# Second feed-forward: the first two feature tiles of the up projection by eight plain products, the differences of token blocks built after them

## The chip, the cores and the metric

The kernel runs on one core of one Trainium2 chip. The core has TensorE (PE, matrix products into PSUM; PEld is its weight load), VectorE (DVE), ScalarE (ACT), GpSimd (POOL) and SyncE (SP, which issues nearly all transfers here). They run side by side, each through its own instructions in order, and wait for one another by semaphores. The metric is device time in microseconds (us).

## The reference

Two layers of a hybrid attention trunk over 1024 latent tokens (plus 256 context tokens) of width 1024: the first with neighbourhood attention, the second with sliding-window attention. Each layer ends with a gated feed-forward with a convolution over positions. In the second layer only the latent tokens pass through it:

```python
def conv_ffn(h, w_up, conv_w, conv_b, w_down):
    u = h @ w_up
    u_p = jnp.pad(u, ((0, 0), (CONV_W // 2, CONV_W // 2), (0, 0)))
    u = sum(u_p[:, tap:tap + t] * conv_w[tap] for tap in range(CONV_W)) + conv_b
    a, g = jnp.split(u, 2, axis=-1)
    return (a * jax.nn.silu(g)) @ w_down
...
h = modulate(rmsnorm(x, g_ffn[i]), sh2, sc2)
x = x + gt2 * conv_ffn(h, ffn_w_up[i], ffn_conv_w[i], ffn_conv_b[i], ffn_w_down[i])
```

D_FF is 2816, so `w_up` has 2 x 2816 columns: 22 feature tiles of 128, each with an `a` and a `g` half.

## The kernel before

**Storage and precision.** Activations lie with the feature on the 128 partitions and tokens along the row: eight slices k of 128 features (0 to 3 are the upper half of the width, 4 to 7 the lower), each 128x512 for one of two token blocks (0: tokens 0 to 511, 1: the rest). Products are made in a reduced format, with each operand split into a high part (a rounded copy, ScalarE) and a low part (the rest, VectorE), and three matmuls for each slice: high by high, high by low, low by high.

**The up projection.** For a feature tile the four results (`a` and `g`, token blocks 0 and 1) are a 2x2 by 2x2 block product: the weights `R["a"]` and `R["g"]` in two halves of 512 rows, and the normalised input in two halves (slices 0 to 3 and 4 to 7) for two token blocks. A plain way takes eight products of 4 slices each. The kernel takes seven, in Strassen's manner (`PROD`, lines 1676 and 1677): it multiplies sums and differences of weight halves by sums and differences of input blocks, and combines the results. In order these are b11, b21, t2, t3, t1, t4, b22; they go into the banks a, d, a, c, a, c, a. `b11` and `b21` are block 0's own two halves; `b22` is block 1's lower half; t1 to t4 are differences (lines 1629 to 1651). Each product is 4 slices x 3 matmuls of 128x512. `plan_up` (from line 1681) also loads the raw weights, forms the four weight sums S1 to S4 (VectorE), splits four weight operands p = 0 to 3 (`plan_w`), copies the first products from PSUM into c0 and c1 (ScalarE), adds the later ones onto them (`out_p`, VectorE), and then forms the convolution (a centre tap on ScalarE, two taps on VectorE for each of g and a), the gate, and combined blocks for the down projection, which go out to DRAM.

**The order.** All work of a feed-forward is handed to a planner (`Sched`, line 61) as operations with an engine, a due key, reads, writes, and claims on rings of buffers. The planner fixes the order on each engine when the kernel is built: among the ready operations the lowest key goes first. A claim in one ring by operations of one class is taken in the order in which the operations were planned. Rings that matter here: `x` (8 buffers of 128x1024: the block 1 input takes 4 of them, c0, c1 and two u the rest), `raw` (3, raw weights from DRAM and the modulation weights `wm`), `w` (4 pairs of split weights), `sr` (4), and 8 banks of PSUM.

**The stretch in question** lies at the start of the second layer's up projection. Ahead of it PE does the attention's output projection (`plan_oproj`) for token block 1; each of the eight results is added to the residual, squared and summed. Then comes the norm of block 1 (`plan_sums`, `plan_bc`: a short chain PE mp, DVE n1v, POOL n1y, DVE n1t, n1y, nsum, PE bc, ACT nsum). `plan_t` multiplies slices by the norm and scale, and lines 1629 to 1663 build t1 to t4 and b22 from both blocks, with high parts on ScalarE and low parts on VectorE (`parts`). Their results lie in tiles t12, t34 and b22. At the same time four steps of the modulation product of the last gate (`plan_mod`, line 354, tile `mod`) are done, with eight loads `wm`. Names in rows: `ua`, `uc`, `ud` are PSUM banks of the up projection, `b1` block 0's split slices, `wraw` raw weights, `whi`/`wlo` split ones, `s` weight sums, `u` and `c` the convolution's tiles.

Of the kernel before, what the change touches and what calls it, by code (L numbers as in the profile page):

```python
# [226 lines left out]
def trunk_kernel(ctx, tc, xperm, xseq, cc, wmod, bmod, gnorm, na_wqkv, na_gq, na_gk, na_bias, na_wo,  # L227
# [3 lines left out]
    act, dve, pool, pe, dma = [InOrder(tc, e) for e in (nc.scalar, nc.vector, nc.gpsimd, nc.tensor, nc.sync)]  # L231
# [35 lines left out]
    dsh = spool.tile([P, 104], F32, name="dsh")[:, :8]  # L267
# [538 lines left out]
    with tc.tile_pool(name="x0", bufs=1, reuse_waits="tile") as xp, \  # L806
# [5 lines left out]
        h = [hi_lo("h0", 0), None, hi_lo("h0", 2)]  # L812
# [4 lines left out]
        for c, parts, key in ((2, 2, 0), (0, 4, 2), (1, 4, 30)):  # L817
            t0, n = CH[c]
# [9 lines left out]
        for kt in range(KT):  # L828
# [110 lines left out]
        for j in range(4):  # L939
# [15 lines left out]
    def ps_alloc(pool_):  # L955
# [6 lines left out]
                bias=3, osb=2, v=8, vc=4, q=8, qc=2, kkc=2, klc=2)  # L962
# [10 lines left out]
    def pair(a):  # L973
# [127 lines left out]
    bias = {}  # L1101
# [158 lines left out]
    FTS = [ft + NP * k for ft in range(NP) for k in range(2)]  # L1260

    def ffn(l, opj, xt1, todo):
        last = l == 1
# [7 lines left out]
        sc = Sched(dict(b=8, raw=3, w=WBUFS, x=8, sr=SRB, g=GB, g2=GB, sq=2), {"b", "raw", "w", "x", "sr", "g", "g2", "sq"})  # L1271
# [22 lines left out]
        LO = {n: ("dve", t_dve(n) + 0.03) for n in (512, 1024)}  # L1294
# [3 lines left out]
        X = [None] * 3  # L1298
# [144 lines left out]
        shift, scale = [modc[:, l, 0, v, :] for v in (3, 4)]  # L1443
        Nm = {}
# [173 lines left out]
        def parts(c, k, hi, lo, tok, key, rel, reads=()):  # L1618
            sc.op("act", t_act(512), lambda e: act.activation(hi(), X[c][:, k, :], AF.Copy), reads=[("x", c, k)] + list(reads),
                  writes=[tok + ("h",)], key=key, rel=rel)  # L1620
            sc.op("dve", t_dve(512), lambda e: sub(e, lo(), X[c][:, k, :], hi().bitcast(F32)), reads=[("x", c, k), tok + ("h",)],
                  writes=[tok + ("l",)], key=key, rel=rel)

        def stt(c, k, c0, k0, s, c1, k1):

            return lambda e: dve.scalar_tensor_tensor(out=X[c][:, k, :], in0=X[c0][:, k0, :], scalar=s, in1=X[c1][:, k1, :],
                                                      op0=ALU.add, op1=ALU.subtract)
        tst = t_dve(512) + 0.06
        for step in range(3):
            for j in range(4):  # L1630
                key = kb + (30.0 * j + 4 * step if not last else 2.0 * j + 8 * step)
                sh = shift[:, j + 4:j + 5]
                if step == 0:
                    plan_t(1, 512, Nm[1], j, xap(1), xtok(1), scale, key)
                    sc.op("dve", t_dve(512), lambda e, j=j: dve.tensor_tensor(
                        out=X[0][:, j, :], in0=X[1][:, j, :], in1=X[0][:, j, :], op=ALU.subtract), reads=[("x", 1, j)],
                        writes=[("x", 0, j)], key=key)
                    parts(0, j, lambda j=j: t12h()[:, 2 * j, :], lambda j=j: t12l(j)[:, 0, :], ("t1", j), key, ())
                elif step == 1:
                    plan_t(1, 512, Nm[1], j + 4, xap(1), xtok(1), scale, key)  # L1640
                    sc.op("dve", tst, stt(0, j, 1, j + 4, sh, 0, j), reads=[("x", 1, j + 4)], writes=[("x", 0, j)], key=key,
                          rel=rx(1, j + 4))
                    parts(0, j, lambda j=j: t12h()[:, 2 * j + 1, :], lambda j=j: t12l(j)[:, 1, :], ("t2", j), key, rx(0, j))
                else:
                    sc.op("dve", tst, stt(1, j, 1, j + 4, dsh[:, j:j + 1], 1, j), reads=[("x", 1, j + 4), ("dsh",)],
                          writes=[("x", 1, j)], key=key, rel=rx(1, j + 4))
                    parts(1, j, lambda j=j: t34_(0)[:, j, :512], lambda j=j: t34_(1)[:, j, :512], ("t3", j), key, rx(1, j), hcs)
                    sc.op("dve", tst, stt(0, j + 4, 0, j + 4, sh, 0, j), reads=[("x", 0, j)], writes=[("x", 0, j + 4)], key=key,
                          rel=rx(0, j))
                    parts(0, j + 4, lambda j=j: t34_(0)[:, j, 512:], lambda j=j: t34_(1)[:, j, 512:], ("t4", j), key, rx(0, j + 4),  # L1650
                          hcs)

        hold = [("hcu",)] if not last else [("t4", j, "l") for j in range(4)]
        sc.op("x", 0.0, lambda e: None, reads=hold, writes=[("hcfree",)], key=-100)
        for j in range(4):
            key = kb + (30.0 * j + 12 if not last else 2.0 * j + 24)
# [4 lines left out]
            sc.op("dve", tst, lambda e, j=j, k=k: dve.scalar_tensor_tensor(  # L1661
                out=b2l()[:, j, :], in0=X[1][:, k, :], scalar=shift[:, k:k + 1], in1=b2h()[:, j, :].bitcast(F32), op0=ALU.add,
                op1=ALU.subtract), reads=[("x", 1, k), ("b2", j, "h")], writes=[("b2", j, "l")], key=key, rel=rx(1, k))

        BP = dict(
            b11=(lambda j: (b1h()[:, j, :], b1l(j // 2)[:, j % 2, :]), lambda j: ("b1", j)),
# [1 line left out]
            b22=(lambda j: (b2h()[:, j, :], b2l()[:, j, :]), lambda j: ("b2", j)),  # L1670
            t1=(lambda j: (t12h()[:, 2 * j, :], t12l(j)[:, 0, :]), lambda j: ("t1", j)),
            t2=(lambda j: (t12h()[:, 2 * j + 1, :], t12l(j)[:, 1, :]), lambda j: ("t2", j)),
            t3=(lambda j: (t34_(0)[:, j, :512], t34_(1)[:, j, :512]), lambda j: ("t3", j)),
            t4=(lambda j: (t34_(0)[:, j, 512:], t34_(1)[:, j, 512:]), lambda j: ("t4", j)))

# [5 lines left out]
        def plan_up(pos):  # L1681
# [33 lines left out]
            ra, rg = T("r", "a"), T("r", "g")  # L1715

            sc.op(*ADD, lambda e: s_op(e, 1, 0, True, lambda: R["g"][:, :512], lambda: R["g"][:, 512:], ALU.add),
                  reads=[rg],
# [953 lines left out]
```

## Time and profile before

| | us |
|---|---|
| median of 3 runs (2808.72 to 2809.52) | 2808.81 |
| the profiled execution | 2809.03 |
| its span on the core | 2807.3 |
| second up projection, first product at | 2147.68 |
| first product of the down projection behind it at | 2587.74 |

Times in rows are us from the start of the span. "Busy" of PE counts matmuls from issue to a modelled end, so that successive ones overlap; the distance of two starts is the real price. Nearly every row carries L51, the line of the helper that records each operation, so rows are told apart by tiles.

### The profile page before, as it was taken

To read this page: it belongs to the slowest core of one execution; us is meant where nothing else is said; L and a number is where in the kernel's file an instruction comes from. 1 tells how busy PE (TensorE), PEld (TensorE's weight loads), DVE (VectorE), ACT (ScalarE), POOL (GpSimd) and SP (SyncE) were. 2 spreads that over 40 slices of the span, in tenths; PEclk is the share of its full clock that TensorE was granted. 3 is DMA by queue.
4 is the path that set the end of the run, shared out by engine and by line. 5 is a ranking of instruction groups with operands and counts; after the bars stand their busy time and mean duration, and the time that the engine had idled before them with its cause. 6 is when DMAs were issued, how large, how long until landed. Compare 5 with 4: busy or idle time off the path is not lost.

```text
span 2807.3 us, 45623 instructions
## 1 busy us (share of the span) xinstructions
PE 2755.6 (98%) x16205; PEld 2426.1 (86%) x16205; DVE 2281.2 (81%) x4990; ACT 1689.7 (60%) x3315; POOL 413.6 (15%) x675
## 2 busy tenths in 40 slices
PE   6999999999999999999999999999999999999999
PEld 5999999999889987777788879999987788888887
DVE  7888878889688687877787688888988888888757
ACT  5877777778456554445454457888864555545443
POOL 1222212223000000000000007645430000000000
PEclk9999999999999999999999999999999999999999
DMA  6232222224645543444466561100253332334745
GB/s 251 65 98 81 66 76 83 89 77 136 242 143 188 187 166 134 161 147 145 152 226 224 166 222 39 30 18 20 82 203 131 121 109 94 113 112 143 251 150 180
DMA packets 144293, 373.52 MB, mean 133 GB/s; under 512 B 22080, under 2 KB 35008, under 8 KB 142656
## 3 DMA queue, kind: packets, MB, share of 16 engines
q1 hardware_dynamic: 144064, 370.60, 39.5%
q8 instruction: 127, 2.08, 0.3%
q14 instruction: 102, 0.84, 0.1%
HBM read 303.50 MB, written 67.04 MB: 132 GB/s over the span
## 4 chain that ended last, share of the span: by engine, by line
PE 70%; DVE 3%; ACT 1%; DMA 1%; issue 1%; POOL 0%; DVEq 0%; SPq 0%; ACTq 0%
PE ua L51 17%; PE dn L51 15%; PE uc L51 13%; PE mm L51 6%; PE ud L51 4%; PE oacc L51 4%; PE pt L51 3%; PE pv L51 3%; PE s L51 2%; PE dnc L51 2%; PE mod L51 1%; DVE S L51 1%; DVE x L51 0%; DVE wlo L51 0%; DVE ptlo L51 0%
## 5 line engine op out<-in xcount | busy, mean ns | idle before, releaser
L51 ACT ACTIVATE whi<-wraw 128x512 fp32r<-128x512 f32 (+1 forms) x264 | 212.3, 805 | 202.6 <-PE uc L51 61.5
L51 DVE TENSOR_TENSOR wlo<-wraw,whi 128x512 fp32r<-128x512 f32 (+1 forms) x264 | 239.3, 908 | 45.2 <-ACT whi L51 44.6
L51 DVE TENSOR_TENSOR ptlo<-pt,pthi 128x512 fp32r<-128x512 f32 (+2 forms) x384 | 223.4, 596 | 56.2 <-ACT pthi L51 53.1
L51 PE MATMUL dn<-ghi,whi 128*128 128x512 f32 x616 | 243.8, 396 | 0.0
L51 PE MATMUL dn<-ghi,wlo 128*128 128x512 f32 x616 | 242.8, 394 | 0.0
L51 PE MATMUL dn<-glo,whi 128*128 128x512 f32 x616 | 242.0, 393 | 0.0
L51 ACT ACTIVATE S<-S,m 128x640 f32<-128x640 f32 (+3 forms) x288 | 221.0, 769 | 26.4 <-DVE m L51 22.6
L51 ACT ACTIVATE pthi<-pt 128x512 fp32r<-128x512 f32 (+2 forms) x384 | 195.3, 524 | 65.0 <-PE pt L51 57.3
L51 DVE SCALAR_TENSOR_TENSOR u<-c,cv,u 128x1023 f32<-128x1023 f32 x176 | 223.2, 1280 | 6.9 <-ACT u L51 5.8
L51 ACT ACTIVATE whi<-s 128x1024 fp32r<-128x1024 f32 (+1 forms) x120 | 113.1, 943 | 190.8 <-PE uc L51 137.2
L51 ACT ACTIVATE ghi<-graw 128x512 fp32r<-128x512 f32 x154 | 96.4, 630 | 192.2 <-PE dn L51 112.5
L51 PE MATMUL pt<-idr,S 128*128 128x128 f32 x1280 | 194.6, 273 | 2.4 <-DVE ptlo L51 1.0
L51 PE MATMUL mm<-whi,h0hi 128*128 128x384 f32 x512 | 181.6, 355 | 0.4 <-ACT qraw L51 0.4
L51 DVE TENSOR_TENSOR glo<-graw,ghi 128x512 fp32r<-128x512 f32 x154 | 105.5, 688 | 82.9 <-ACT ghi L51 76.5
L51 PE MATMUL mm<-wlo,h0hi 128*128 128x384 f32 x512 | 172.3, 337 | 0.0
L51 DVE TENSOR_TENSOR wlo<-s,whi 128x1024 fp32r<-128x1024 f32 (+1 forms) x120 | 129.6, 1080 | 42.4 <-ACT whi L51 42.2
L51 PEld LDWEIGHTS pt<-idr,S 128*128 128x128 f32 x1280 | 151.0, 140 | 10.0 <-DVE ptlo L51 1.7
L51 POOL TENSOR_TENSOR n1y<-n1v,mhalf 128x4 f32<-128x4 f32 (+1 forms) x9 | 9.2, 1024 | 934.7 <-DVE n1v L51 934.7
L51 PE MATMUL ua<-t12hi,whi 128*128 128x512 f32 x352 | 138.7, 394 | 5.5 <-ACT t12hi L51 4.0
L51 POOL TENSOR_TENSOR qy<-qv,mhalf 128x4 f32<-128x4 f32 (+1 forms) x112 | 119.6, 1069 | 149.4 <-DVE qv L51 129.3
L51 PEld LDWEIGHTS dn<-ghi,wlo 128*128 128x128 f32 x616 | 115.5, 187 | 28.4
L51 PEld LDWEIGHTS dn<-glo,whi 128*128 128x128 f32 x616 | 115.5, 188 | 27.4
(353 smaller groups left out, 8767.0 us busy)
## 6 DMA issues: line engine op xcount, KB each, us to landing
wraw<-in_w_up_dram SPq DMA_DIRECT2D x132, 512.0 KB, 3.5
wm<-in_wmod_dram SPq DMA_DIRECT2D x80, 512.0 KB, 4.1
wraw<-in_w_down_dram SPq DMA_DIRECT2D x44, 512.0 KB, 3.6
graw<-g_dram SPq DMA_DIRECT2D x44, 512.0 KB, 4.5
wraw<-in_w_down_dram SPq DMA_DIRECT2D x88, 256.0 KB, 3.1
graw<-g_dram SPq DMA_DIRECT2D x66, 256.0 KB, 2.8
slab<-in_na_wqkv_dram SPq DMA_DIRECT2D x32, 384.0 KB, 3.7
woraw<-in_na_wo_dram SPq DMA_DIRECT2D x24, 512.0 KB, 4.0
```

Of the source, the lines that this page charges most:

```text
L51: r = f(*a, **k)
```

## The change

It affects the second layer only (`PLAIN = 2 if last else 0`). Tiles 0 and 1 (`pos < PLAIN`) are made by eight plain products, four banks U[s, n] (s: a or g; n: token block), with two raw weights split whole and no sums of weights; each result leaves PSUM by one copy on ScalarE and there are no additions onto c. The products of block 0 (n = 0) read b11 and b21 as before. Those of block 1 (n = 1) read new split slices `e` of block 1, which `early` writes into the tiles of t3 and t4. The differences are planned after these two tiles, with keys later by 8; t3 and t4 wait until the last plain products have read `e` (`done`). The normalisation of block 1's slices moves from the differences into `early`. `plan_u`, the convolution and what follows, is the old code as a function of its own.

```diff
-        for step in range(3):
+        PLAIN = 2 if last else 0
+        done = [[("up", FTS[p], "done", h, j) for p in range(PLAIN) for j in range(4)] for h in range(2)]
+
+        def early(h, key):
             for j in range(4):
...
+                k = 4 * h + j
+                cs = slice(512 - 512 * h, 1024 - 512 * h)
+                plan_t(1, 512, Nm[1], k, xap(1), xtok(1), scale, key + j)
+                sc.op("act", t_act(512), lambda e, j=j, k=k, cs=cs: act.activation(
+                    t34_(0)[:, j, cs], X[1][:, k, :], AF.Identity, bias=shift[:, k:k + 1]),
+                    reads=[("x", 1, k)], writes=[("e", h, j, "h")], key=key + j)
+                sc.op("dve", tst, lambda e, j=j, k=k, cs=cs: dve.scalar_tensor_tensor(
+                    out=t34_(1)[:, j, cs], in0=X[1][:, k, :], scalar=shift[:, k:k + 1], in1=t34_(0)[:, j, cs].bitcast(F32),
+                    op0=ALU.add, op1=ALU.subtract), reads=[("x", 1, k), ("e", h, j, "h")], writes=[("e", h, j, "l")], key=key + j)
...
+        if PLAIN:
+            early(0, kb)
+            early(1, kb + 4)
+        def plan_diffs():
+            for step in range(3):
+                for j in range(4):
+                    key = kb + (30.0 * j + 4 * step if not last else 2.0 * j + 8 * step + 8 * (PLAIN > 0))
...
+                        parts(1, j, lambda j=j: t34_(0)[:, j, :512], lambda j=j: t34_(1)[:, j, :512], ("t3", j), key, rx(1, j), hcs + done[1])
...
+                        parts(0, j + 4, lambda j=j: t34_(0)[:, j, 512:], lambda j=j: t34_(1)[:, j, 512:], ("t4", j), key, rx(0, j + 4),
+                              hcs + done[0])
...
-                sc.op("dma", 1.8, load, writes=[T("r", s)], key=pk - 8, acq=[("raw", T("r", s), 5 if s == "a" else 4)])
+                sc.op("dma", 1.8, load, writes=[T("r", s)], key=pk - 8, acq=[("raw", T("r", s), 2 if pos < PLAIN else 5 if s == "a" else 4)])
...
+            if pos < PLAIN:
+                for p, r, s in ((0, ra, "a"), (3, rg, "g")):
+                    w = ("up0" if p == 0 else "up", ft, "w", p)
+                    sc.op("act", t_act(1024), whi(p, lambda s=s: R[s], 1024), reads=[r], writes=[T("w", p, "h")], key=pk + p,
+                          acq=[("w", w, 16)], rel=[r])
+                    sc.op(*LO[1024], wlo(p, lambda s=s: R[s], 1024), reads=[r, T("w", p, "h")], writes=[T("w", p, "l")], key=pk + p,
+                          rel=[r])
+                U, C = {}, {}
+                for n in range(2):
+                    for kh in range(2):
+                        for s in range(2):
+                            p = 3 * s
+                            ap, tok = BP[f"e{kh}" if n else f"b{kh + 1}1"]
+                            for j in range(4):
+                                def mm(e, s=s, p=p, kh=kh, n=n, j=j, ap=ap):
+                                    if kh == 0 and j == 0:
+                                        U[s, n] = bank(f"u{s}{n}")
+                                    hi, lo = ap(j)
+                                    ws = slice(512 * kh + j * P, 512 * kh + (j + 1) * P)
+                                    for m, (w, x) in enumerate(((0, hi), (0, lo), (1, hi))):
+                                        pe.matmul(U[s, n], W[p][w][:, ws], x, start=(kh == 0 and j == 0 and m == 0),
+                                                  stop=(kh == 1 and j == 3 and m == 2))
+                                tk = tok(j)
+                                sc.op("pe", 3 * t5, mm, reads=[T("w", p, "h"), T("w", p, "l"), tk + ("h",), tk + ("l",)],
+                                      writes=[T("u", s, n)] + ([T("done", kh, j)] if s and n else []),
+                                      key=key + (2.72 * (2 * kh + s) if n == 0 else 10.9 + 5.44 * kh + 1.36 * j + 0.68 * s),
+                                      acq=[("b", ("u", s, n, ft), 1)] if kh == 0 and j == 0 else (),
+                                      rel=[("up0" if p == 0 else "up", ft, "w", p)])
+                    for s in range(2):
+                        def out(e, s=s, n=n):
+                            if n == 0:
+                                C[str(s)] = x_tile("c" + str(s))
+                            act.activation(C[str(s)][:, 512 * n:512 * n + 512], U[s, n], AF.Copy)
+                        sc.op("act", t_actp(512), out, reads=[T("u", s, n)], writes=[T("c", 2 * s + n)], key=key - 30,
+                              acq=[("x", T("ct", s), 3)] if n == 0 else (), rel=[("u", s, n, ft)])
+                plan_u(pos, ft, key, C, T)
+                return
...
+            plan_u(pos, ft, key, C, T)
+
+        def plan_u(pos, ft, key, C, T):
             V = {}
...
         for pos in range(FT):
+            if pos == PLAIN:
+                plan_diffs()
             plan_up(pos)
```

More of the change, by code (lines that the diff above doesn't have):

```diff
@@ L1653, in ffn @@
[L1653 to L1656, printed above, removed]
+                k = 4 * h + j
[4 more added lines that the diff above has]
+                    reads=[("x", 1, k)], writes=[("e", h, j, "h")], key=key + j)
@@ L1657, in ffn, with b22 @@
+                sc.op("dve", tst, lambda e, j=j, k=k, cs=cs: dve.scalar_tensor_tensor(
+                    out=t34_(1)[:, j, cs], in0=X[1][:, k, :], scalar=shift[:, k:k + 1], in1=t34_(0)[:, j, cs].bitcast(F32),
+                    op0=ALU.add, op1=ALU.subtract), reads=[("x", 1, k), ("e", h, j, "h")], writes=[("e", h, j, "l")], key=key + j)
+        def b22(j, key):
             k = j + 4
@@ L1663, in ffn @@
                 op1=ALU.subtract), reads=[("x", 1, k), ("b2", j, "h")], writes=[("b2", j, "l")], key=key, rel=rx(1, k))
+        if PLAIN:
[5 more added lines that the diff above has]
+                    key = kb + (30.0 * j + 4 * step if not last else 2.0 * j + 8 * step + 8 * (PLAIN > 0))
+                    sh = shift[:, j + 4:j + 5]
+                    if step == 0:
+                        if not PLAIN:
+                            plan_t(1, 512, Nm[1], j, xap(1), xtok(1), scale, key)
+                        sc.op("dve", t_dve(512), lambda e, j=j: dve.tensor_tensor(
+                            out=X[0][:, j, :], in0=X[1][:, j, :], in1=X[0][:, j, :], op=ALU.subtract), reads=[("x", 1, j)],
+                            writes=[("x", 0, j)], key=key)
+                        parts(0, j, lambda j=j: t12h()[:, 2 * j, :], lambda j=j: t12l(j)[:, 0, :], ("t1", j), key, ())
+                    elif step == 1:
+                        if not PLAIN:
+                            plan_t(1, 512, Nm[1], j + 4, xap(1), xtok(1), scale, key)
+                        sc.op("dve", tst, stt(0, j, 1, j + 4, sh, 0, j), reads=[("x", 1, j + 4)], writes=[("x", 0, j)], key=key,
+                              rel=rx(1, j + 4))
+                        parts(0, j, lambda j=j: t12h()[:, 2 * j + 1, :], lambda j=j: t12l(j)[:, 1, :], ("t2", j), key, rx(0, j))
+                    else:
+                        sc.op("dve", tst, stt(1, j, 1, j + 4, dsh[:, j:j + 1], 1, j), reads=[("x", 1, j + 4), ("dsh",)],
+                              writes=[("x", 1, j)], key=key, rel=rx(1, j + 4))
+                        parts(1, j, lambda j=j: t34_(0)[:, j, :512], lambda j=j: t34_(1)[:, j, :512], ("t3", j), key, rx(1, j), hcs + done[1])
+                        sc.op("dve", tst, stt(0, j + 4, 0, j + 4, sh, 0, j), reads=[("x", 0, j)], writes=[("x", 0, j + 4)], key=key,
+                              rel=rx(0, j))
+                        parts(0, j + 4, lambda j=j: t34_(0)[:, j, 512:], lambda j=j: t34_(1)[:, j, 512:], ("t4", j), key, rx(0, j + 4),
+                              hcs + done[0])
+            sc.op("x", 0.0, lambda e: None, reads=[("hcu",)] if not last else [("t4", j, "l") for j in range(4)],
+                  writes=[("hcfree",)], key=-100)
+            for j in range(4):
+                b22(j, kb + (30.0 * j + 12 if not last else 2.0 * j + 24))
@@ L1715, in plan_up @@
             ra, rg = T("r", "a"), T("r", "g")
+            if pos < PLAIN:
[11 more added lines that the diff above has]
+                            ap, tok = BP[f"e{kh}" if n else f"b{kh + 1}1"]
+                            for j in range(4):
+                                def mm(e, s=s, p=p, kh=kh, n=n, j=j, ap=ap):
[21 more added lines that the diff above has]
+                return
```

23 lines of the change are left out of this document (2 added, 21 removed).

## The prediction

> **What bounds the kernel now.** I read the page's first part, then stretches of the second feed-forward's start, then TensorE's waits there.
>
> ```profile
> span 2807.3 us, 45623 instructions
> PE 2755.6 (98%) x16205; PEld 2426.1 (86%) x16205; DVE 2281.2 (81%) x4990; ACT 1689.7 (60%) x3315; POOL 413.6 (15%) x675
> ```
>
> PE is busy for 98% of the span, so only a place where PE waits, or fewer products, can shorten it. The next view cuts the up projection of the second layer into stretches (columns: stretch, length, then busy time and instructions of PE, PEld, DVE, ACT, POOL; granted clock; DMA share; GB/s).
>
> ```profile
> 2147.68:2156.16 8.48, 7.43 (x41) 6.13 (x40) 5.65 (x15) 2.92 (x4) 1.01 (x1) 1.00 0.38 125
> 2156.16:2162.10 5.94, 5.85 (x27) 4.33 (x25) 5.78 (x10) 1.77 (x3) 0.00 (x0) 1.00 0.28 91
> 2162.10:2167.20 5.10, 1.15 (x17) 0.42 (x16) 5.10 (x9) 2.84 (x4) 0.00 (x0) 0.92 0.60 198
> 2167.20:2176.70 9.50, 8.51 (x29) 4.34 (x30) 9.50 (x16) 3.15 (x5) 0.00 (x0) 0.51 0.24 74
> 2176.70:2191.60 14.90, 14.90 (x77) 11.39 (x75) 13.36 (x21) 9.93 (x15) 0.00 (x0) 1.00 0.31 101
> 2191.60:2198.70 7.10, 4.42 (x31) 2.86 (x31) 6.32 (x7) 5.88 (x7) 0.00 (x0) 1.00 0.62 214
> 2207.10:2226.14 19.04, 19.04 (x86) 15.77 (x85) 17.51 (x21) 10.04 (x13) 0.00 (x0) 1.00 0.34 125
> 2226.14:2587.70 361.56, 361.56 (x1597) 299.49 (x1596) 298.45 (x346) 184.70 (x225) 0.00 (x0) 1.00 0.31 109
> ```
>
> The seventh row is one feature tile of seven products: 19.04 us, so 2.72 a product. From 2207 on PE is full. Ahead of that it is not, and in the third and fourth rows DVE is busy for all 14.6 us: it builds the differences of token blocks that the products t2, t3, t1, t4 need. The clock there is 0.51. TensorE's waits in this place name the chain:
>
> ```profile
> PE ua L51 <- ACT t12hi L51: 4.0, 1, 4.0
> PE ua L51 <- ACT c L51: 1.4, 1, 1.4
> PE mod L51 <- ACT modsb L51: 1.2, 1, 1.2
> PE bc L51 <- DVE nsum L51: 1.0, 1, 1.0
> PE ua L51 <- DVE t12lo L51: 0.9, 2, 0.5
> ```
>
> PE's timeline has the ends of the stage and what lies in it besides products (start, duration, engine, line, operation, then idle time ahead and its releaser):
>
> ```profile
> 2147.68 0.39 PE L51 MATMUL ua<-b1hi,whi 128*128 128x512 f32 x1
> ...
> 2151.09 0.95 PE L51 MATMUL mp<-invd,nsum 128*128 128x1 f32 x8
> 2151.90 0.48 PE L51 MATMUL ud<-b1hi,whi 128*128 128x512 f32 x1
> ...
> 2155.25 1.16 PE L51 MATMUL bc<-nsum,ones 128*128 128x128 f32 x8 [1.05 <-DVE nsum L51]
> 2156.16 0.48 PE L51 MATMUL ua<-b1hi,whi 128*128 128x512 f32 x1
> ...
> 2162.18 1.07 PE L51 MATMUL mod<-wm,cpad 128*32 128x256 f32 x16
> ...
> 2167.21 0.79 PE L51 MATMUL ua<-t12hi,whi 128*128 128x512 f32 x1 [3.96 <-ACT t12hi L51]
> ...
> 2587.74 0.40 PE L51 MATMUL dn<-ghi,whi 128*128 128x512 f32 x1
> ```
>
> The up projection runs from 2147.68 to 2587.74, 440.06 us. 22 tiles of 19.04 are 418.88. The norm's two small steps take 0.81 and 0.91 (start to start of the next), four modulation steps of 1.07 take 4.28, their transpose some 0.2 (my estimate): 6.2. What is left, 440.06 - 418.88 - 6.2 = 15.0 us, is loss, all ahead of 2198.7. Its pieces: 4.0 waiting for t12hi; in the fourth row 9.5 us in which only 12 product matmuls (2.72) and one modulation step (1.07) ran, so 5.7 lost to the clock and two waits for t12lo; 1.4 for c; 1.2 for modsb; 1.0 for nsum; 1.7 in small change. These 15.0 us are all that the change can win.
>
> **The change, part by part.** Removed from tiles 0 and 1: the seven products each on differences. Added: eight plain ones each. The first four (n=0) need only token block 0 and the raw weights, which are split before 2147.68 or soon after; the other four (n=1) need the eight slices e of block 1. So PE has 2 x 8 x 2.72 = 43.52 us instead of 38.08: **+5.44 us**, on the path for certain.
>
> What it buys is order. DVE's prices, from the same stretch and from the steady one (line, engine, operation, shapes, count, busy, mean ns, idle ahead), and its pitch from two successive starts:
>
> ```profile
> L51 DVE SCALAR_TENSOR_TENSOR x<-x,modc,x 128x512 f32<-128x512 f32 x8 | 5.9, 742 | 0.0
> L51 DVE TENSOR_TENSOR t12lo<-x,t12hi 128x512 fp32r<-128x512 f32 x8 | 5.2, 682 | 0.0
> L51 DVE SCALAR_TENSOR_TENSOR b22lo<-x,modc,b22hi 128x512 fp32r<-128x512 f32 x4 | 2.8, 748 | 0.1
> L51 DVE SCALAR_TENSOR_TENSOR u<-c,cv,u 128x1023 f32<-128x1023 f32 x76 | 96.3, 1279 | 0.1
> L51 DVE TENSOR_TENSOR u<-u 128x1024 f32<-128x1024 f32 x19 | 23.1, 1218 | 0.1
> ...
> 2157.08 1.41 DVE L51 SCALAR_TENSOR_TENSOR x<-x,modc,nsum 128x512 f32<-128x512 f32 x2 [0.16 <-ACT nsum L51]
> 2158.41 1.29 DVE L51 TENSOR_TENSOR x<-x,x 128x512 f32<-128x512 f32 x2
> 2159.61 0.74 DVE L51 SCALAR_TENSOR_TENSOR x<-x,modc,nsum 128x512 f32<-128x512 f32 x1
> ```
>
> Two of the three-operand form take 1.33 start to start, two of the plain form 1.20: 0.66 and 0.60 each. By the same overlap of about 0.08 a 1024-wide one is 1.14 and a tap of the convolution 1.20.
>
> *The slices e.* Eight normalisations and eight low parts, 16 x 0.66 = 10.6 us of DVE from 2157.1 to 2167.7; ScalarE's eight high parts run beside them. They stand first by their keys (46 to 53, against 54 to 78 for the differences). PE reaches them after 10.88 us of n=0 products, 1.72 of norm steps, and the wait for nsum: about 2161.6, or 2162.7 with one modulation step. The first slice is there by about 2160.2 (one normalisation, ScalarE's 0.63 as for the 128x512 split below, one low part, two hand-overs). DVE delivers a slice every 1.33 us and PE uses one every 1.36: no wait. The 4.0 and the 5.7 go.
>
> *Tile 1's n=0* is another 10.88 us that needs no difference, so the differences have from 2167.7 until tile 1's end, T1. T1 is 2147.68 + 43.52 + 6.2 + waits of about 1.5 = 2198.9.
>
> *DVE's bill from 2167.7 to T1*, 31.2 us: first differences and t1 low parts 8 x 0.60 = 4.8; t2 with low parts 4 x (0.66 + 0.60) = 5.0; tile 0's four taps, product and one block 4 x 1.20 + 1.14 + 0.60 = 6.5; of tile 2's weights two low parts and four sums 2 x 1.14 + 4 x 0.60 = 4.7; the eight sums for t3 and t4 5.3. That is 26.3, or 28.7 with t4's low parts. It fits, at some 90% of DVE's time. Against this the plain tiles spare DVE eight weight sums, two weight splits, and six additions onto c; these were on no path of PE's.
>
> *The added wait.* t3 and t4 take the same tile as e1 and e0, so their high parts wait on ScalarE for the last n=1 products ("done"): t4 from 5.44 us before T1, t3 from T1 on. Behind T1 tile 2 wants t3 at T1 + 8.16, t4 at 13.6, b22 at 16.3. There DVE owes t3's low parts 2.4, tile 1's taps 4.8, one weight split 1.14, an addition 0.60: 8.9 us from about T1 + 1.3, done by T1 + 10.2 at worst with t3's first slices earlier. Then b22 2.65, tile 1's product and three blocks 2.9, one split 0.60: 16.4. Nearly in time, nothing over.
>
> *The x ring* is what is late next. Block 1's four buffers of eight are kept until t3 and b22 are split, now behind T1; tile 1 has the other four (c0, c1 and two u). Tile 2's c0 must be copied out before its third product may go on in the same bank, at T1 + 5.44. A buffer comes free when tile 1's first part has had both taps. ScalarE's prices here:
>
> ```profile
> 2188.84 0.63 ACT L51 ACTIVATE whi<-wraw 128x512 fp32r<-128x512 f32 x1 [1.29 <-PE uc L51]
> 2189.79 1.24 ACT L51 ACTIVATE u<-c,cv 128x1024 f32<-128x1024 f32 x1 [0.32 <-DVE c L51]
> 2191.79 0.60 ACT L51 ACTIVATE c<-ua 128x512 f32<-128x512 f32 x1 [0.75 <-PE ua L51]
> ```
>
> Copy of the last bank done at T1 + 1.5 (one weight split in front of it), the centre tap to 3.2, two taps on DVE to 5.8, copy of tile 2's c0 to 6.4, PE at 6.7: 1.3 late. One slice of t3 (0.68) can fill part. I take 0.9; bounds are 0 (the order there lets the copy through) and 3.5 (second centre and both parts' taps stand in front).
>
> *Waits that stay:* nsum 1.0, as that chain is not changed, with 0.2 about it; bounds 0.6 (the addition onto c that stood in the chain is gone) and 1.2. modsb 1.2 is an order that the planner may or may not repeat: 0.6, bounds 0 and 1.2. Small change 0.3, bounds 0 and 1.7. The loads I cost at nothing: raw buffers of the plain tiles are free after two uses instead of five, so the eight modulation loads, which now begin at 2149.26 and queue for one buffer, get more of them, and tile 2's follow by about 2175, 24 us ahead of T1. If that cover fails PE waits for a load, 3.5 us.
>
> ```profile
> wraw<-in_w_up_dram SPq DMA_DIRECT2D x132, 512.0 KB, 3.5
> ...
> 2139.96 0.33 SPq L51 DMA_DIRECT2D wraw<-in_w_up_dram  x1
> ...
> 2149.26 36.54 SPq L51 DMA_DIRECT2D wm<-in_wmod_dram  x8
> ```
>
> **Sum:** 15.0 - 5.44 - (1.2 + 0.6 + 0.9 + 0.3 = 3.0) = 6.6 us won. From the profiled execution's 2809.03 that gives 2802.4; the median of the runs is 0.22 lower, so **2802.2 us**. The best case by the lower bounds (0.6 left) wins 9.0: 2799.8. From 2198 on PE waits for nothing, so what is won there arrives at the end whole.
>
> The 0.51 of the fourth stretch follows the idle 3.96 us, while the other waits, up to 1.4 us, left the clock at 1.00. The Trainium skill, "TensorE: Matmul & The Clock Gate", Part 1, says that the array falls to half speed after about one idle window of 3.4 us and wants one such window of work to come back. The trace agrees as to 0.51 and to the side of 3.4 on which each wait lies; by that page a wait of 1 or 2 us behind T1 costs itself alone, and one past 3.4 brings a slow stretch along; the page alone changes no term of the sum.
>
> **The rivals.**
>
> *The gain is half eaten behind T1.* The x ring and t3 cost their upper 3.5, modsb 1.2, small change 1.7, nsum 1.2: 7.6 left in place of 3.0, so 2.0 won: 2806.8. For it: DVE has no slack from 2157 on, and three things wait for tile 1's end at once. Against it: the part that frees the buffer has a low key.
>
> *The stall moves and returns whole (slower).* If DVE's work, 54 us from 2157.1 to b22's low parts at T1 + 16.3 = 2215.2 (10.6 + 26.3 + 8.9 + 2.4 for t4 + 6.2), runs at the steady stretch's 298.45/361.56 = 83% instead of 93%, it takes 65 us, 7 us too long. PE then waits 7 in tile 2, which is longer than the 3.96 that was followed by a slow stretch losing 5.7. Left: 3.0 - 0.9 + 7 + 5.7 = 14.8; with the 5.44 that is 20.2 against 15.0 before: 2814.0. It becomes slower than before once the new wait, with its slow stretch, passes 15.0 - 5.44 - 2.1 = 7.5, so already from one unbroken wait of about 4. For it: in-order engines and a 90% bill. Against it: DVE was busy 14.6 of 14.6 us in the old stall, so it can run dense, and the 83% of the steady stretch is lack of work.
>
> *The cover is not there.* Tile 1's banks are claimed after tile 0's in a fixed turn, so PE can't slip tile 1's n=0 in front of a late slice. If DVE puts weight splits of tile 1 (2 x 1.14) and other things in front of the slices, PE waits some 4 at 2162 and falls to the slow clock again: 4.0 + 5.7 + 3.0 left = 12.7, 18.1 with the products, 3.1 slower: 2811.9. Against it: keys 46 to 53 stand ahead of nearly everything but those splits, and their raw weights land by about 2143.5 (2139.96 + 3.5).
>
> **How the numbers follow.** A measurement of this kernel tells 0.2%, 5.6 us, from no change: below 2803.2 is faster, above 2814.4 slower. The forecast has 0.55 (its own range 2799.8 to 2804.5), the half-eaten gain 0.22, the stall moved behind T1 0.16, the missing cover 0.07. Faster takes nearly all of the forecast and a little of the second: 0.55. Slower takes about half of the last two, as their sizes are open above: 0.12. The rest, 0.33, is no change. For eight in ten I leave out the slower half of the two bad cases and a little at the lower end: 2799.7 to 2811.5.
>
> **What will show it.** Right: about 2162 to 2188 PE runs with clock 1.00, no wait for t12hi, b22 or e above 1 us; the first dn starts near 2581; DVE above 90% from 2157 to T1 near 2199; a wait of about 1 for c behind T1. Wrong: a wait of PE of 3 us or more on t34h, t34l or c between T1 and T1 + 20, with a clock near 0.5 after it; or PE idle at 2162 on e's parts; or T1 later than 2202. The prediction falls if tile 2 or 3 still loses more than 4 us.

## The result and the profile after

Measured side by side on one chip, the kernel before takes 2810.18 us (median of 15 runs, 2807.58 to 2812.31) and the changed one 2805.08 us (median of 15, 2802.90 to 2809.62): ratio 0.9984, 95% interval 0.9977 to 0.9991, about 4.5 us less by the ratio and 5.1 by the medians. The interval excludes no change, though the gain stays inside the 0.2% that the prediction set as its bound. A second measurement of the same two kernels on another chip gave 2807.18 against 2810.21, ratio 0.9988 (0.9979 to 0.9997).

The profiled execution took 2805.87 us. Its page begins (span; busy time, share and instructions by engine):

```profile
span 2804.1 us, 45680 instructions
PE 2758.0 (98%) x16229; PEld 2429.4 (87%) x16229; DVE 2274.3 (81%) x4980; ACT 1690.7 (60%) x3319; POOL 412.8 (15%) x675
```

PE has 24 matmuls more, DVE ten instructions fewer, and the span is 3.2 us shorter. The stage is found as before, from the first product to the first dn, in PE's timeline (columns as in the prediction):

```profile
2149.27 0.39 PE L51 MATMUL u<-b1hi,whi 128*128 128x512 f32 x1
...
2154.23 1.07 PE L51 MATMUL mod<-wm,cpad 128*32 128x256 f32 x16
...
2158.09 1.05 PE L51 MATMUL bc<-nsum,ones 128*128 128x128 f32 x8
...
2164.18 0.50 PE L51 MATMUL u<-t34h,whi 128*128 128x512 f32 x1
...
2174.44 0.39 PE L51 MATMUL u<-b1hi,whi 128*128 128x512 f32 x1
...
2202.30 0.39 PE L51 MATMUL u<-t34h,wlo 128*128 128x512 f32 x1
...
2205.25 0.39 PE L51 MATMUL ua<-b1hi,whi 128*128 128x512 f32 x1
...
2211.51 0.50 PE L51 MATMUL ua<-t12hi,whi 128*128 128x512 f32 x1 [0.66 <-ACT c L51]
...
2221.72 0.50 PE L51 MATMUL uc<-t34h,wlo 128*128 128x512 f32 x1 [0.60 <-DVE wlo L51]
...
2230.55 0.50 PE L51 MATMUL ua<-b1hi,wlo 128*128 128x512 f32 x1 [0.38 <-DVE wlo L51]
2231.53 0.49 PE L51 MATMUL ua<-t12hi,whi 128*128 128x512 f32 x1 [0.47 <-ACT c L51]
...
2584.59 0.40 PE L51 MATMUL dn<-ghi,whi 128*128 128x512 f32 x1
```

Neither `mod` nor `bc` has an idle time ahead of it, and the slices e (read from the tile t34h, from 2164.18 to 2202.53) come without a wait. At 2174.44 PE runs tile 1's products of token block 0 between tile 0's e products. The four waits that remain all lie behind tile 1. The same in stretches (stretch, length, busy time and instructions of PE, PEld, DVE, ACT, POOL; granted clock; DMA share; GB/s):

```profile
2149.27:2164.18 14.91, 14.91 (x97) 11.52 (x95) 8.47 (x18) 5.22 (x8) 1.01 (x1) 1.00 0.43 142
2164.18:2202.53 38.35, 38.35 (x195) 30.23 (x192) 36.69 (x55) 20.95 (x30) 0.00 (x0) 1.00 0.33 110
2202.53:2231.53 29.00, 26.77 (x113) 20.34 (x111) 27.88 (x35) 19.24 (x27) 0.00 (x0) 1.00 0.29 100
2231.53:2584.59 353.06, 353.06 (x1557) 292.33 (x1558) 293.10 (x339) 181.67 (x220) 0.00 (x0) 1.00 0.31 110
```

The clock is 1.00 throughout, and PE is full to the end of tile 1 and again from 2231.53. In the third row it is not, and there DVE is busy for 27.88 of 29.00 us: the place of the shortage has moved from the differences (2162 to 2177 before) to the work behind tile 1. ScalarE is dense at the head of it too, 13.26 of 13.38 us from 2201.82 to 2215.20.

The stage takes 2584.59 - 2149.27 = 435.32 us against 440.06, so 4.74 were won. I account for it as the prediction did, in matmuls start to start (19.04 us of a seven-product tile by 84 matmuls: 0.2267 each):

| us | predicted | before | after |
|---|---|---|---|
| product matmuls (1848; 1872) | +5.44 | 418.9 | 424.4 |
| mp, bc, four mod steps, transpose | 0 | 6.2 | 5.8 |
| loss, all else | from 15.0 to 3.0 | 15.0 | 5.1 |
| stage | -6.6 | 440.06 | 435.32 |

The prediction's terms give 5.44 - 12.0 = -6.6 for the stage; measured are -4.74. The span moved by only 3.2 because this execution entered the stage 1.59 us later (2149.27 against 2147.68); what follows the first dn is 219.5 us in both. The kernels below were profiled once each (the changed one twice) and timed beside the kernel before; the stage is the sharper measure, as the time ahead of it varies from execution to execution (last section).

### The profile page after: what moved, and what is told of

Read it like the earlier page. It is cut to its first block, busy times and chain, and to the rows that moved or that the text cites. A ratio compares the mean times of both kernels' runs of the same rounds, so it can differ in the third digit from the quotient of the medians.

```text
span 2804.1 us, 45680 instructions
## 1 busy us (share of the span) xinstructions
PE 2758.0 (98%) x16229; PEld 2429.4 (87%) x16229; DVE 2274.3 (81%) x4980; ACT 1690.7 (60%) x3319; POOL 412.8 (15%) x675
## 5 line engine op out<-in xcount | busy, mean ns | idle before, releaser
L51 PEld LDWEIGHTS dn<-ghi,whi 128*128 128x128 f32 x616 | 115.6, 188 | 26.8
```

What stands on the lines that cost most here:

```text
L51: r = f(*a, **k)
```

## The experiments

The theory to be tested: the slices e give VectorE the time that it needs, the old stall and its slow stretch go, and the 5.1 us left are VectorE's debt behind tile 1. Its rivals are named in each expectation.

| kernel | stage | loss | median | ratio to before, 95% |
|---|---|---|---|---|
| before | 440.06 | 15.0 | 2810.18 | |
| after | 435.32 | 5.1 | 2805.08 | 0.9984 (0.9977 to 0.9991) |
| plain1 | 445.81 | 18.3 | 2814.83 | 1.0015 (1.0006 to 1.0024) |
| plain3 | 436.65 | 3.7 | 2806.87 | 0.9992 (0.9984 to 1.0001) |
| reuse | 434.43 | 4.2 | 2805.44 | 0.9986 (0.9977 to 0.9995) |
| warm | 439.44 | | 2808.60 | 0.9997 (0.9988 to 1.0006) |
| nokey | 433.09 | 2.9 | 2803.75 | 0.9979 (0.9970 to 0.9988) |
| dveback | 435.49 | 5.3 | 2804.56 | 0.9983 (0.9974 to 0.9991) |
| late4 | 437.38 | 7.2 | 2807.55 | 0.9993 (0.9984 to 1.0002) |
| both | 431.34 | 1.1 | 2801.29 | 0.9965 (0.9953 to 0.9978) |

The kernel before had 2809.46 us beside plain1, plain3, reuse and warm, 2809.58 beside nokey, dveback and late4, and 2810.21 beside both. Loss is the stage less 0.2267 for each product matmul and less 5.8 for the small steps (for the kernel before 6.2, as the prediction has it; there the waits behind two of the steps hide their pitch). All edits are against the changed kernel, except that of warm.

**One plain tile (plain1) and three (plain3).**

```diff
-        PLAIN = 2 if last else 0
+        PLAIN = 1 if last else 0
```

> One plain tile instead of two. Theory A (the plain products win by being a cover as long as VectorE's bill): the cover is 21.8 us from 2149, the bill up to tile 1's t3 is 38 us from 2158 with tile 0's taps and tile 1's weights, so PE waits 5 to 10 us in tile 1, part of it at a clock near 0.5; loss in the stage 10 to 16, products +2.72, time 2807 to 2813. Rival (each plain tile wins by itself, through the work it spares VectorE): about half of the gain of two tiles with 2.72 in place of 5.44 paid, loss near 10, time near 2807, no single wait above 3 us and no slow clock.

PE's longest wait in total (us, times, longest), the ScalarE copy that ends the first of the three, and the stretches about the two long ones:

```profile
PE ua L51 <- ACT c L51: 7.3, 3, 3.3
```

```profile
2186.51 0.60 ACT L51 ACTIVATE c<-ua 128x512 f32<-128x512 f32 x1 [1.64 <-DVE u L51]
```

```profile
2182.60:2187.20 4.60, 1.25 (x18) 0.32 (x17) 4.57 (x5) 2.94 (x6) 0.00 (x0) 1.00 0.67 248
2187.20:2190.00 2.80, 2.10 (x7) 1.21 (x8) 2.10 (x4) 2.79 (x4) 0.00 (x0) 0.71 0.40 157
2190.00:2198.60 8.60, 7.85 (x19) 5.73 (x19) 8.60 (x15) 3.53 (x6) 0.00 (x0) 0.50 0.30 107
2216.60:2220.00 3.40, 0.33 (x2) 0.00 (x0) 3.25 (x4) 3.34 (x6) 0.00 (x0) 0.87 0.47 154
2220.00:2225.60 5.60, 5.50 (x13) 4.34 (x14) 4.79 (x5) 1.40 (x3) 0.00 (x0) 0.50 0.28 94
```

With one tile the products cost 2.72 less than with two, yet the stage is 5.75 longer than before the change; loss and time lie beyond what was expected. PE stands still while DVE is busy for 4.57 of 4.60 us, then for 3.25 of 3.40, and each time runs at half clock afterwards. The first copy into c had itself waited for VectorE's taps (u). At the second ScalarE is busy too, for 3.34 of 3.40 us, so the row doesn't tell which of the two was late. This is the outcome that the prediction's slower rival described, a long wait with a slow stretch behind it, though its cause there was a VectorE that runs less densely; here it is dense, and one tile is too short a cover for its debt.

> Three plain tiles. Theory A (a price of 2.72 us on the path for each tile, and a loss of 4.0 behind the cover that more cover reduces): products 2.72 us longer than with two, loss of the stage 2 to 4 instead of 5.2, time 0 to 1.7 us above the changed kernel, 2805 to 2807. Rival (the loss behind the cover comes with the change from plain to seven products and only moves): loss 5, time 2.7 above, 2808.

The edit is the same with 3. The stage was 1.33 longer than with two: 2.72 for the third tile, less 1.4 of loss. Two waits are left, both for c and behind the last plain tile:

```profile
PE ua L51 <- ACT c L51: 2.0, 2, 1.4
```

So two is the better number here, and the loss doesn't go away with a third.

**Slow clock or VectorE (warm, on the kernel before).** Eighteen spare matmuls, whose result nobody reads, are put into the old 4.0 us wait.

```diff
+        if last:
+            for i in range(18):
+                def warm(e, i=i):
...
+                    pe.matmul(WB[0], b1h()[:, 0, :P], b1h()[:, 0, :], start=True, stop=True)
+                sc.op("pe", t5, warm, reads=[("up", FTS[1], "u", "d"), ("b1", 0, "h")], writes=[("warm",)], key=1e6 + i,
```

> The kernel before, with 18 spare matmuls of 128x512 on block 0's first slice (result never read) in PE's old wait for t12hi. It tells what the slow clock cost by itself in the 9.5 us at 0.51. As the prediction costed it (5.7 us lost to clock and two waits of 0.9 in all): the clock stays at 1.00 and 3 us come back, time 2806 to 2807. Rival (VectorE's differences set the pace there, the slow clock is hidden behind them): granted clock 1.00, the waits for t12lo grow in its place, time within 1.5 us of before.

```profile
2162.30:2167.20 4.90, 4.90 (x34) 3.36 (x33) 4.90 (x8) 2.73 (x4) 0.00 (x0) 1.00 0.30 67
2167.20:2176.70 9.50, 6.96 (x37) 3.68 (x35) 9.50 (x16) 3.74 (x8) 0.00 (x0) 1.00 0.50 176
```

PE is now busy through the old wait and the clock stays at 1.00 in the next 9.50 us, where it was 0.51. The stage gets only 0.62 shorter, and 1.8 us of waits for t12lo turn up, against 0.9 before. DVE is busy for 14.40 of these 14.40 us, as it was for 14.6 of 14.6: it set the pace, and the half clock lay mostly under it.

**What the remaining loss is (late4, dveback, reuse, nokey).** late4 adds VectorE work behind tile 1's last product: twelve additions of 128x128, 2.4 us together, whose result nobody reads.

```diff
+                    for i in range(12):
+                        sc.op("dve", t_dve(128), lambda e, i=i: dve.tensor_tensor(out=spare(), in0=b1h()[:, i % 4, :P].bitcast(F32),
+                              in1=b1h()[:, i % 4 + 4, :P].bitcast(F32), op=ALU.add), reads=[("spare",)], writes=[("spare1",)], key=58)
```

> The changed kernel with twelve small VectorE additions more (128x128, some 0.2 us each, 2.4 us in all, never read) that are due as soon as tile 1's last product is done. In the changed kernel PE loses about 4 us between 2205 and 2235. Theory A (VectorE's debt behind tile 1 sets that loss): it grows by 1.5 to 2.5, stage 436.8 to 437.8. Rival (it is set by the order of copies into c and the x ring, VectorE has slack between): it grows by less than 0.7.

```profile
PE uc L51 <- DVE t34l L51: 1.6, 2, 1.3
PE ua L51 <- ACT c L51: 1.1, 2, 0.7
PE uc L51 <- DVE wlo L51: 0.6, 1, 0.6
PE ua L51 <- DVE wlo L51: 0.4, 1, 0.4
```

The last three rows are those of the changed kernel; the first is new. 2.4 us of VectorE work made the stage 2.06 longer, nearly one for one: behind tile 1 VectorE has no slack.

dveback puts back the eight sums of weights which the plain tiles spare; nobody reads them.

```diff
             if pos < PLAIN:
+                for i, (t, c, x, y, op, rd, rl) in enumerate((
+                        (1, 0, lambda: R["g"][:, :512], lambda: R["g"][:, 512:], ALU.add, [rg], [rg]),
...
+                    sc.op(*ADD, lambda e, t=t, c=c, x=x, y=y, op=op: s_op(e, t, c, c == 0, x, y, op), reads=rd,
```

> The changed kernel with the eight weight sums of the two plain tiles put back on VectorE (8 x 0.60 = 4.8 us; nothing reads them). Theory A (what the plain tiles spare VectorE lay on no path of PE's, as it falls before 2157 where VectorE waits anyway): stage within 0.5 us of 435.3. Rival (the spared work is part of the gain): stage 1 to 4 us longer, with new waits of PE for wlo or e.

The edit also counts the uses of the raw weights as the kernel before does. VectorE does the last of them here:

```profile
2146.46 0.69 DVE L51 TENSOR_TENSOR s<-wraw,s 128x512 f32<-128x512 f32 x1
```

That is just before the stage's first product (2146.76 in this run). The stage was 435.49 against 435.32, and the waits are those of the changed kernel to within 0.1. 8 x 0.60 = 4.8 us of VectorE's work ahead of the stage change nothing in it, 2.4 behind tile 1 cost 2.06.

reuse takes work away behind tile 1: e1 is block 1's lower half, which is also what b22 needs, so b22 is read from e1's place, and t3 goes into b22's tiles.

```diff
+                if PLAIN:
+                    parts(1, j, lambda j=j: b2h()[:, j, :], lambda j=j: b2l()[:, j, :], ("t3", j), kb + 2.0 * j + 24, rx(1, j), [("hcfree",)])
+                    continue
...
+        if PLAIN:
+            BP["t3"] = (BP["b22"][0], BP["t3"][1])
+            BP["b22"] = BP["e1"]
```

> The changed kernel with one more step: the split slices e1 serve as b22 for all later tiles, t3 is put into the buffers that b22 had, and so no b22 is built (4 ScalarE and 4 VectorE operations of 0.66 us fewer, 2.65 us of DVE) and t3 no longer waits for the end of tile 1. In the changed kernel PE loses 5.2 us in the stage beside products, modulation and norm steps, 4.0 of it between 2210 and 2232. Theory A (what is left is VectorE's debt behind tile 1 and the gate on t3): the loss between 2205 and 2235 falls to 1.5 or less, the time to about 2802, 2.5 to 3.5 us below the changed kernel. Theory B (what is left comes from c, the x ring and the weights of tiles 2 to 4, whatever the differences do): the loss stays near 4 and the time within 1 us of the changed kernel.

Four high and four low parts are not made, and t3 no longer waits for tile 1's last products. The stage was 0.9 shorter, with 1.1 us of waiting for c and 0.7 for weights left. Theory A had asked for 2.5 to 3.5 us, so this is theory B's outcome: the conflict on t3's tile was not the main thing, and taking 2.65 us off VectorE did not come back one for one.

nokey drops the delay of 8 in the differences' keys.

```diff
-                    key = kb + (30.0 * j + 4 * step if not last else 2.0 * j + 8 * step + 8 * (PLAIN > 0))
+                    key = kb + (30.0 * j + 4 * step if not last else 2.0 * j + 8 * step)
```

> The changed kernel with the differences' keys not moved by 8, so that on VectorE the eight first differences and t1's low parts (4.8 us) mix with the slices e, which are done 4.8 us later. Theory A (the slices must stand first, as the prediction has it; PE has about 2 us in hand there): PE waits 2 us or more for e's parts between 2160 and 2178, stage 437 to 438 instead of 435.3, time 2807 to 2808. Rival (tile 1's block 0 products, which PE already mixes into tile 0's block 1 products at 2174 in the changed kernel, fill in): no such wait above 0.5, stage 434.8 to 435.8.

The stage was 2.2 us shorter than the changed kernel's, better than either theory had it, and the slices e still come without a wait. VectorE's order about the end of tile 1, the changed kernel:

```profile
2200.56 0.68 DVE L51 TENSOR_TENSOR s<-wraw 128x512 f32<-128x512 f32 x1
2201.27 0.69 DVE L51 TENSOR_TENSOR s<-s,wraw 128x512 f32<-128x512 f32 x1
...
2203.68 2.37 DVE L51 TENSOR_TENSOR wlo<-s,whi 128x1024 fp32r<-128x1024 f32 x2
2205.97 4.86 DVE L51 SCALAR_TENSOR_TENSOR u<-c,cv,u 128x1023 f32<-128x1023 f32 x4
...
2218.52 0.75 DVE L51 SCALAR_TENSOR_TENSOR b22lo<-x,modc,b22hi 128x512 fp32r<-128x512 f32 x1
2219.18 0.69 DVE L51 TENSOR_TENSOR t34l<-x,t34h 128x512 fp32r<-128x512 f32 x1
2219.78 0.74 DVE L51 SCALAR_TENSOR_TENSOR b22lo<-x,modc,b22hi 128x512 fp32r<-128x512 f32 x1
2220.45 2.35 DVE L51 TENSOR_TENSOR wlo<-s,whi 128x1024 fp32r<-128x1024 f32 x2
```

nokey:

```profile
2199.68 0.69 DVE L51 TENSOR_TENSOR s<-wraw 128x512 f32<-128x512 f32 x1
2200.40 0.69 DVE L51 TENSOR_TENSOR s<-s,wraw 128x512 f32<-128x512 f32 x1
2201.01 2.07 DVE L51 SCALAR_TENSOR_TENSOR b22lo<-x,modc,b22hi 128x512 fp32r<-128x512 f32 x3
2203.00 0.68 DVE L51 TENSOR_TENSOR s<-wraw 128x512 f32<-128x512 f32 x1
...
2219.24 2.36 DVE L51 TENSOR_TENSOR wlo<-s,whi 128x1024 fp32r<-128x1024 f32 x2
```

With the later keys tile 3's four weight sums (the first two shown; tile 2's four were done by 2193.7) run at the end of tile 1, and b22's and t34's low parts pile up to 2220.45, just ahead of the split weights for which PE waits at 2221.72. Without the delay three of the four sums still run there, but three of b22's low parts stand among them and are done by 2203.1, and PE waits for no weights, only for c (two waits, 1.1 us in all).

ScalarE shows a second difference, in the copy of tile 2's first result into c. The changed kernel, then nokey:

```profile
2210.26 0.71 ACT L51 ACTIVATE b22hi<-x,modc 128x512 fp32r<-128x512 f32 x1
2210.88 0.58 ACT L51 ACTIVATE c<-ua 128x512 f32<-128x512 f32 x1
```

```profile
2205.34 0.59 ACT L51 ACTIVATE c<-ua 128x512 f32<-128x512 f32 x1
```

That is 61.6 us after the stage's first product, behind tile 1's taps, against 57.5, when the taps begin. The same copy comes at 57.7 in reuse, 57.9 in both and 61.6 in late4. In nokey, reuse and both block 1's slices are done with sooner, which fits a buffer of the x ring that comes free sooner. No run moves that alone, so the 2.2 us are not divided between VectorE's order and the x ring.

**reuse and nokey together (both).**

> The two edits that shortened the stage, together: e1 serves as b22 with t3 in b22's old buffers (alone 434.4 us for the stage against 435.3), and the differences' keys not moved by 8 (alone 433.1). The fixed part of the stage is 430.2 (products 424.3, norm and modulation 5.9), and some 1.2 of loss lies around the small matmuls and stays. Theory A (both cut VectorE's debt behind tile 1, which the one with twelve additions showed to count nearly one to one): stage 431.5 to 432.7, time about 2803 on a chip where before takes 2809.5. Rival (the keys already took what there was, the rest is the copy into c behind the x ring): 433.0 to 433.5.

```profile
2147.08:2161.99 14.91, 14.91 (x97) 11.53 (x95) 8.46 (x18) 5.14 (x8) 1.01 (x1) 1.00 0.42 142
2161.99:2200.34 38.35, 38.35 (x194) 30.24 (x191) 36.81 (x55) 22.25 (x33) 0.00 (x0) 1.00 0.32 110
2200.34:2229.34 29.00, 29.00 (x129) 24.03 (x128) 28.71 (x33) 18.84 (x25) 0.00 (x0) 1.00 0.30 108
2229.34:2578.42 349.08, 349.08 (x1541) 289.13 (x1540) 287.62 (x333) 174.88 (x212) 0.00 (x0) 1.00 0.31 110
```

In the third row PE is busy for 29.00 of 29.00 us (26.77 in the changed kernel), and the profile shows no wait of PE anywhere in the stage. It takes 431.34 us, of which 1.1 is neither a product nor a small step. The median was 2801.29 us (5 runs, 2799.53 to 2801.73), ratio 0.9965 (0.9953 to 0.9978); the changed kernel was timed on the same chip:

> The changed kernel once more, beside the one with both edits on the same chip, for a comparison of their times and for a second profile of its stage: 435.3 us again within 0.3 if the stage's loss is set by the order of work, and a start of the stage that may differ by 1 to 2 us, as nothing ahead of it was changed on PE. If the stage itself varies by more than 0.5, the differences of under 1 us between the kernels here are not to be read.

It gave 2807.18, ratio 0.9988 (0.9979 to 0.9997), and the stage again 435.32. The two intervals don't overlap, so this version beats both kernels. What it wins over the changed kernel's stage, 3.98 us, is more than reuse (0.89) and nokey (2.23) win alone, 3.12 together.

## Why the prediction was right or wrong

The direction was right, and so was the mechanism of the gain; of the terms that remain several were not. The time came out 2.9 us above the 2802.2 forecast and inside the range, but above the forecast's own 2799.8 to 2804.5 and, by the prediction's bound of 2803.2, in "no change", which had 0.33 against 0.55 for faster; 1.4 of that is the kernel before, which had 2810.18 beside it where the forecast started from 2808.81, the rest a smaller gain (5.1 by medians, 4.74 in the stage, for 6.6).

- **The two extra products, +5.44.** 24 matmuls more at 0.2267: exact. plain1 and plain3 are reckoned at the same pitch.
- **The wait for t12hi and the slow stretch go.** They did: PE full and the clock at 1.00 from 2149.27 to 2202.53. But the step "5.7 lost to the clock and two waits for t12lo" named the wrong cause for most of it. warm kept the clock at 1.00 and won 0.6; VectorE's full bill lay under the slow products. The sum is not touched by this, since the change takes away both.
- **No wait for e; the end of tile 1.** Tile 1's last e product ends at 2202.53, 53.26 us after the stage's start, 2.72 of it tile 2's first product drawn ahead: 50.5, where 2198.9 - 2147.68 = 51.2 was forecast.
- **"They stand first by their keys", and the missing cover.** nokey shows that the slices e need no delay of the differences. The prediction also held that PE can't put tile 1's products in front of a late slice; the row at 2174.44 shows that it does. Both reasons were too cautious, and the delay of 8, which the prediction used and did not cost, takes 2.2 us.
- **VectorE's spared sums on no path.** dveback, 0.17 us: right for the eight sums. The spared splits and additions were not put back.
- **nsum 1.2 and modsb 0.6 stay.** Neither did; a modulation step ran at 2154.23 inside the norm's chain, and the `bc` and `mod` rows have no idle time ahead of them. 1.8 better than forecast.
- **c and the x ring, 0.9.** The place was right (2211.51, 0.66 idle, 0.82 by matmul starts), and the size in part luck. The copy was forecast for T1 + 5.8, 57.0 us after the stage's start, and came at 61.6, with no idle time of ScalarE ahead of it: t34h and b22hi stand in front. PE would have stood still from 2205.25 on, had it not drawn tile 3's first two products ahead, 5.44 us, where the prediction saw 0.68 to fill with. A second wait of 0.75 at 2231.53 makes it 1.57. Whether an earlier place on ScalarE alone would shorten these waits was not tested.
- **"Nearly in time, nothing over" behind tile 1, and the weights at nothing.** This is the step that failed. The forecast had b22 done at T1 + 16.4; the last b22lo ends 2219.78 + 0.74 = 2220.5, which is T1 + 18.0 (from the stage's start 71.2 where 67.6 was forecast, as T1 here has tile 2's first product in front of it), and two splits of weight sums stand behind it (2220.45). What the bill left out are tile 3's weights: their four sums, from 2200.56 on, come in front of tile 1's taps. Two waits for wlo came, 0.77 and 0.53 by matmul starts, 1.30 where nothing was put; the first is for split sums (2220.45), the second for split raw weights, which VectorE starts only at 2229.27. How much of it the four sums make is not shown: three of them stand there in nokey too, without a wait for weights. late4 shows that work added to VectorE there counts nearly one for one. reuse and nokey bring the loss down, but the copy into c comes sooner in both as well.
- **Small change 0.3.** 5.1 - 1.57 - 1.30 = 2.2 remain, of which about 1.1 also stand in both, where nothing waits. The lower bound of 0 was too low.

Left were thus 0 + 0 + 1.6 + 1.3 + 2.2 = 5.1 in place of 3.0: 1.8 forecast and not met set off 3.9 met and not forecast, so the sum came nearer than its terms. The sign by which the prediction would fall, more than 4 us lost in tile 2 or 3, was only just missed: from 2202.53 to 2234.39, 31.86 us, PE ran 123 product matmuls, 27.88, so 3.98 were lost. The half-eaten gain had the right mechanism for the miss (VectorE without slack, several things due at tile 1's end), at less than half its size. The rival on the slower side did not decide with two plain tiles; plain1 shows that such a stall can come back. In place of one unbroken wait of about 4 with a slow stretch behind there were two, of 3.35 and 3.16.

## What to carry to other kernels

When an engine's backlog stalls PE, products that need none of its results are worth their price if they last as long as the backlog; too short a cover cost more than none here, and the third tile brought back 1.4 of its 2.72. Behind the cover list everything that was put off, with the buffers that it holds and the next tiles' weights, and look for results that the cover already made and that serve again. A delay written into the order to protect the cover has to be costed like any other step.

## What the runs showed of the hardware

**A half clock can cost nearly nothing.** Before the change 9.5 us ran at 0.51; with the clock held at 1.00 (warm) the stage was 0.62 us shorter, since VectorE set the pace. The granted clock alone is no price; the engine that feeds the products has to be looked at in the same row.

**What brings the half clock.** Its two cases in plain1 follow waits of 3.35 and 3.16 us:

```profile
2187.16 0.50 PE L51 MATMUL ua<-t12hi,whi 128*128 128x512 f32 x1 [3.35 <-ACT c L51]
...
2220.10 0.79 PE L51 MATMUL ua<-t12hi,whi 128*128 128x512 f32 x1 [3.16 <-ACT c L51]
```

After the first the clock was still 0.71 on the mean of the next 2.80 us and 0.50 for 8.60 after that; after the second it was at 0.50 from 2220.00 on for 5.60 us. The wait of 1.4 us for c before the change left it at 1.00. The Trainium skill, "TensorE: Matmul & The Clock Gate", Part 1, puts the drop after at least one idle window of about 3.4 us. The trace agrees roughly; the 3.16 us show that a wait slightly under that length can do it, so a forecast shouldn't count on that margin.

The length of the wait alone does not decide. In finer stretches of plain1 the clock falls in the middle of the second wait:

```profile
2218.60:2219.10 0.50, 0.00 (x0) 0.00 (x0) 0.50 (x1) 0.50 (x1) 0.00 (x0) 1.00 0.32 123
2219.10:2219.60 0.50, 0.00 (x0) 0.00 (x0) 0.50 (x2) 0.50 (x2) 0.00 (x0) 0.51 0.00 0
```

That is 2.2 us after the wait began, while the first fall, at 2188.4, comes 1.2 us after its wait had ended. The clock comes back at 2198.6 and at 2225.9; before the change it falls at 2166.3 and comes back at 2176.6. From a fall to its return are 10.2, 6.8 and 10.2 us, from plain1's first fall to its second 30.7: 3, 2, 3 and 9 times 3.41. So in these two traces the clock changes on a beat that does not start with the wait, and in plain1 the 3.41 us ahead of each fall still held about 1.2 us of matmuls (an estimate from these times). Nothing here was built to test that beat.

**A floor of about 1.1 us.** both has no wait of PE in the stage, and still 1.1 us more than its matmuls and small steps by their pitch, in pieces of about 0.1 where PE changes between 128x512 products and the small ones. What makes these was not looked into.

**The time ahead of the stage moves by microseconds.** PE's instructions up to the stage are the same in the kernels before and after, and yet the stage began at 2149.27 in one profile of the changed kernel and at 2152.02 in the other. Over all profiles the ends are dveback, where VectorE has eight sums more ahead of the stage, and that second profile:

```profile
2146.76 0.39 PE L51 MATMUL u<-b1hi,whi 128*128 128x512 f32 x1
```

```profile
2152.02 0.39 PE L51 MATMUL u<-b1hi,whi 128*128 128x512 f32 x1
```

That is 5.3 us apart, more than the whole gain, and 2.75 for one and the same program, while its stage repeated to the last digit (435.32 twice). A change of this size is read from the stage; for the whole time it takes many runs. Where these microseconds come from was not settled.
